# Gathering the first expert by itself and scattering expert outputs as separate partial rows, in an expert layer of a two-layer diffusion block

## The chip, the cores and the metric

The kernel runs on one core of one Trainium2 chip. The metric is the device time of one execution in microseconds; a time stands for the median of several runs.

## What is computed

Two transformer-like layers run over 256 latent and 256 context tokens of width 1024. Only the channel mixer of the second layer matters here. It is a layer of eight experts, and each of the 256 latent tokens goes to its two best:

```python
def _moe(h, router, w_gate, w_up, w_down):
    logits = (t @ router).astype(jnp.float32)
    top_val, top_idx = lax.top_k(logits, TOP_K)          # TOP_K = 2
    top_w = jax.nn.softmax(top_val, axis=-1)
    gate = jnp.sum(jax.nn.one_hot(top_idx, N_EXPERTS) * top_w[..., None], axis=1)
    for e in range(N_EXPERTS):                           # 8, each 1024 -> 3584 -> 1024
        out = out + gate[:, e:e + 1] * _swiglu(t, w_gate[e], w_up[e], w_down[e])
```

All weights are float32. The weights of the eight experts are 352 MB, and each is read once.

## The kernel before

**Stages.** Layer 0 and the mixer of layer 1 run first. From there on the code that the change touches runs: `prep_tile` (1450) computes router logits and each token's two experts for one tile of 128 tokens (the two latent tiles are `LAT = (0, 1)`); `moe_prep` (1487) computes each token's rank within each expert by matmuls with a strict triangle `tri` and with ones (lines 1495 to 1499, issued by the helper at line 1827), copies the ranks to `rk` (1501), finishes the modulated input `hf` (`modulated`, 1445 and 1448) and builds the first map; `moe_layer` (1964) does the experts; `store` (2005) writes the output.

**Gather and scatter.** `moe_map` (1527) builds, on DVE, a 0/1 map of tokens by slots for an expert: slot n holds the token whose rank is n, up to S = 96 slots. `moe_gather` (1537) handles two experts at a time. In four pieces of two blocks of 128 features it multiplies `hf` (the stationary operand, 128 columns) with the maps of both experts (192 moving columns) into a PSUM bank and copies the result to `xg` on ACT. Then it transposes each expert's map on PE (line 1564) and copies it to `ohT` on DVE (1565); the scatter uses it. A float32 matmul appears in the trace as two instructions, so a gather of 16 matmuls is 32 of them, and a pair of transposes is two.

**The expert loop.** An expert is four units. In a unit `gate_up` (1585) runs two halves of gate and up matmuls, four at a time on 32-column strips of the array (`four`, 1571), `turned` (1613) transposes the result, and `moe_down` (1631) of the unit before follows. Slots 0 to 63 are always computed. The third strip, slots 64 to 95, is computed only if the expert has more than 64 tokens; PE branches on that at run time (`arms`, 1578). So an expert with the third strip has 1.5 times the matmuls of one without. After an expert's last unit, `moe_out` (1651) scales its result into `y`, adding two partial sums for slots 64 to 95, and `moe_add` (1668) splits `y` into a high and a low part (1673, 1674), scatters both by a matmul with `ohT` (1682) and adds the result to `xt` (1684).

**Order of work.** PE's instructions in the loop are in the order of the code. Gathers and scatters wait in the queue `behind`, and `paced` (1972) lets one piece of the queue's head run after each half of `gate_up` and after each `moe_down`. Before the change the gather of experts 2 and 3 runs within expert 1, of 4 and 5 within expert 3, of 6 and 7 within expert 5; that of 0 and 1 runs ahead of the loop. On the other engines a scheduler may move instructions when the kernel is compiled.

**Weights.** `Ring` (161) holds 30 slots of 512 KB. Its loads go through SP's DMA queue, which has at most eight transfers on their way: an issue waits until the eighth transfer before it has landed. `ring.grow` (1955) issues most of the first 30 loads, as slots come free near the end of the mixer; the second `ring.grow` (1961), after `moe_prep`, issues the last two. From then on a load is issued as soon as PE is done with a slot.

Of the kernel before, what the change touches and what calls it, by code (L numbers as in the profile page):

```python
# [9 lines left out]
F32 = mybir.dt.float32  # L10
# [6 lines left out]
ALU = mybir.AluOpType  # L17
# [179 lines left out]
class Gen:  # L197
# [88 lines left out]
    def load_consts(self, cp, mp):  # L286
# [1163 lines left out]
    def prep_tile(self, tt, ws, ga):  # L1450
# [30 lines left out]
        nc.vector.tensor_copy(ixf[:, tt], ix[:, tt, 0:2])  # L1481
        nc.vector.tensor_scalar(s1[:, tt], self.iota[:, :8], ixf[:, tt, 0:1], None, op0=ALU.is_equal)
        nc.vector.tensor_scalar(o2[:, tt], self.iota[:, :8], ixf[:, tt, 1:2], None, op0=ALU.is_equal)
# [42 lines left out]

    def moe_map(self, e0, ne, sel, rank, n=S):

        oh = self.mem.get(4, [P, 2, ne, n], "oh")
# [7 lines left out]
    def moe_gather(self, e0, ne, out, sel, rank, n=S, oh=None):  # L1537

        nc, mem = self.nc, self.mem
        if oh is None:  # L1540
            oh = self.moe_map(e0, ne, sel, rank, n)
# [4 lines left out]
        o2 = mem.get(4, [P, ne, 256], "ohT", F32R)  # L1546
        left = [ne]
        for d in range(0, KD, 2):
            yield from self.avail("t")
            ps = self.psum("t")  # L1550
            for i in range(2):
                for tt in LAT:
                    self.mm(ps, ps[:, i * w:i * w + w], self.hf[tt][:, (d + i) * P:(d + i) * P + P],
                            oh[:, tt].rearrange("p a b -> p (a b)"), tt == 0, tt == 1)
            v = ps[:, :2 * w].rearrange("p (i j n) -> p i j n", i=2, j=ne)
            for j in range(ne):
                self.act(xg[j][:, d:d + 2], v[:, :, j], AF.Copy)
            self.done(ps)
            yield
        for j in range(ne):  # L1560
            yield from self.avail("t")
            ps = self.psum("t")
            for tt in LAT:
                self.last[id(ps)] = nc.tensor.transpose(ps[:n, tt * P:tt * P + P], oh[:, tt, j], self.ident)
            nc.vector.tensor_copy(o2[:n, j], ps[:n, :256])
            self.done(ps)
            out[e0 + j] = xg[j], o2[:, j], (o2, left)
            yield
        mem.put(oh)
# [61 lines left out]
    def moe_down(self, e, hT, u, yb, yx):  # L1631

        m = 4 if u < 3 else 2
        w = [(t[:, :512], t[:, 512:]) for t in self.ring.need(2 * m)]
        for arm in self.arms(e):
            if u == 0 and not arm:
                self.four(yx, 512, ((self.zero, w[0][0]),) * 4, True, True)
            for j in range(m):
                v = w[2 * j:2 * j + 2]
                for i, (w0, w1) in enumerate(v):  # L1640
                    b0, b1 = hT[:, j, i, :32], hT[:, j, i, 32:64]
                    self.four(yb, 512, ((b0, w0), (b1, w0), (b0, w1), (b1, w1)), u == 0 and j == 0 and i == 0,
                              u == 3 and j == 1 and i == 1)
                xa, xb = hT[:, j, 0, 64:], hT[:, j, 1, 64:]
                if arm:
                    self.four(yx, 512, ((xa, v[0][0]), (xa, v[0][1]), (xb, v[1][0]), (xb, v[1][1])),
                              u == 0 and j == 0, u == 3 and j == 1)
        yield
        self.mem.put(hT)

    def moe_out(self, yb, yx):

        nc, mem, gf = self.nc, self.mem, self.gf
        y, t = mem.get(4, [P, 2, 512], "y"), mem.get(4, [P, 2, 512], "yt")
        for dh in range(2):
# [3 lines left out]
        self.act(y[64:S, 1], yx[32:64], AF.Copy)  # L1659
        self.act(t[64:S, 1], yx[96:], AF.Copy)  # L1660
        nc.vector.tensor_tensor(y[64:S, 0], yx[64:S], y[64:S, 0], op=ALU.add)
        nc.vector.tensor_tensor(y[64:S, 1], t[64:S, 1], y[64:S, 1], op=ALU.add)
        self.done(yb, yx)
        nc.vector.tensor_tensor(y[64:S], y[64:S], gf[64:S].rearrange("p (a b) -> p a b", a=2), op=ALU.mult)
        mem.put(t)
        return y

    def moe_add(self, y, o, gate, n=S, free=None):
# [24 lines left out]

    def moe_rest(self):

        nc, tc = self.nc, self.tc
        with tc.For_i(0, NE, 1) as e:
            for off, n in ((S, P), (S + P, 256 - S - P)):
                with tc.If(nc.values_load(self.cnt[0:1, bass.ds(e, 1)], min_val=0, max_val=256) > off):
                    self.moe_rest_expert(bass.ds(e, 1), off, n)  # L1700

    def moe_rest_expert(self, one, off, n):
# [6 lines left out]
        xg = {}  # L1709
        self.run(self.moe_gather(0, 1, xg, *cols[:2], n))  # L1710
        x, o, free = xg[0]
# [124 lines left out]
    def build(self):  # L1836
        nc, tc, A = self.nc, self.tc, self.A
        with ExitStack() as ctx:
# [125 lines left out]
    def moe_layer(self):  # L1964
# [13 lines left out]
        def lower():  # L1978
# [5 lines left out]
            if u == 3:  # L1984
                behind.append(self.moe_add(self.moe_out(*y), xg[e][1], self.gate[:, :, e:e + 1], S, xg[e][2]))
# [19 lines left out]
    def store(self):  # L2005
        for tt in LAT:
            for z in range(2):
                s = slice(512 * z, 512 * z + 512)
# [27 lines left out]
def _consts():  # L2036
# [5 lines left out]
    for lv in range(7):  # L2042
# [75 lines left out]
```

## Time and profile before

| | |
|---|---|
| runs | 1835.87, 1839.38, 1839.55 us; median 1839.38 |
| the profiled execution | 1835.17 us |
| its span, first to last instruction | 1833.4 us |
| before the first expert matmul | 936.3 us |
| expert loop, first to last expert matmul | 878.9 us |
| after the last expert matmul | 18.2 us |

PE is TensorE's matmuls, PEld its weight loads, DVE is VectorE, ACT is ScalarE, SP is the engine that issues the DMAs. Times of the trace count from the span's start. The granted clock is the share of 2.4 GHz that TensorE got.

### The profile page before, as it was taken

To read this page: it belongs to the slowest core of one execution; us is meant where nothing else is said; L and a number is where in the kernel's file an instruction comes from. 1 tells how busy PE (TensorE), PEld (TensorE's weight loads), DVE (VectorE), ACT (ScalarE), POOL (GpSimd) and SP (SyncE) were. 2 spreads that over 40 slices of the span, in tenths; PEclk is the share of its full clock that TensorE was granted. 3 is DMA by queue.
4 is the path that set the end of the run, shared out by engine and by line. 5 is a ranking of instruction groups with operands and counts; after the bars stand their busy time and mean duration, and the time that the engine had idled before them with its cause. 6 is when DMAs were issued, how large, how long until landed. Compare 5 with 4: busy or idle time off the path is not lost. (4 is left out here: it accounts for less than half of the span.)

```text
span 1833.4 us, 34728 instructions
## 1 busy us (share of the span) xinstructions
PE 1753.2 (96%) x14056; PEld 1084.3 (59%) x14057; DVE 778.5 (42%) x1924; ACT 537.7 (29%) x1203; POOL 33.3 (2%) x56
## 2 busy tenths in 40 slices
PE   6999999999999999999989998999989999999996
PEld 3999778988788898998843333333333333333332
DVE  4656877899755377868720011110212011120112
ACT  4654655723223256765410010100101011010100
POOL 1000000100000001000000000000000000000000
PEclk9999999999999999999989999999999999999998
DMA  9224342366763245230589999999999999999990
GB/s 347 73 83 147 114 150 80 117 241 226 240 221 134 97 143 182 89 127 13 196 316 379 402 406 407 406 407 400 402 400 406 404 402 402 400 407 404 403 392 31
DMA packets 137006, 485.64 MB, mean 265 GB/s; under 512 B 15888, under 2 KB 17040, under 8 KB 136784
## 3 DMA queue, kind: packets, MB, share of 16 engines
q1 hardware_dynamic: 136080, 480.08, 69.1%
q8 instruction: 168, 2.75, 0.6%
q0 software_dynamic: 704, 2.36, 0.4%
q14 instruction: 54, 0.44, 0.1%
HBM read 481.33 MB, written 1.05 MB: 263 GB/s over the span
## 5 line engine op out<-in xcount | busy, mean ns | idle before, releaser
L1575 PE MATMUL u<-wr,xg 128*32 128x512 f32 (+1 forms) x5376 | 523.9, 545 | 19.7 <-issue 14.6
L1575 PEld LDWEIGHTS u<-wr,xg 128*32 128x32 f32 x5376 | 174.0, 111 | 342.2 <-issue 291.5
L1575 PE MATMUL mm<-wr,mT 128*32 128x512 f32 x2352 | 261.1, 593 | 3.8 <-ACT mh L264 1.5
L125 ACT ACTIVATE hi<-raw 128x512 fp32r<-128x512 f32 (+2 forms) x296 | 160.3, 580 | 247.1 <-PE u L246 84.8
L126 DVE TENSOR_TENSOR lo<-raw,hi 128x512 fp32r<-128x512 f32 (+2 forms) x296 | 178.9, 636 | 98.3 <-ACT hi L125 96.7
L1608 DVE TENSOR_TENSOR mh<-mh,u 128x512 f32<-128x512 f32 (+1 forms) x32 | 19.8, 619 | 410.9 <-PE u L1575 257.0
L1575 PEld LDWEIGHTS mm<-wr,mT 128*32 128x32 f32 x2352 | 77.8, 110 | 175.4 <-issue 149.7
L264 ACT ACTIVATE mh<-u 128x512 f32<-128x512 f32 (+1 forms) x64 | 34.6, 540 | 413.9 <-PE u L1575 413.3
L244 PE MATMUL u<-hx,hi 128*128 128x512 f32 (+1 forms) x384 | 142.9, 372 | 0.0
L245 PE MATMUL u<-hx,lo 128*128 128x512 f32 (+1 forms) x384 | 142.7, 372 | 0.0
L246 PE MATMUL u<-hx,hi 128*128 128x512 f32 (+1 forms) x384 | 142.7, 372 | 0.0
L264 ACT ACTIVATE mT<-t 128x512 f32<-128x512 f32 (+1 forms) x32 | 17.4, 544 | 256.3 <-PE t L1620 255.4
L245 PE MATMUL mm<-fx,lo 128*128 128x256 f32 (+1 forms) x264 | 85.7, 325 | 4.4 <-DVE lo L126 4.2
L244 PE MATMUL mm<-hi,hx 128*128 128x256 f32 x288 | 85.3, 297 | 4.2 <-ACT hx L264 3.9
L244 PE MATMUL mm<-fx,hi 128*128 128x256 f32 (+1 forms) x264 | 85.0, 322 | 0.6 <-ACT hi L125 0.6
L1626 DVE COPY mT<-t 128x256 f32<-128x256 f32 (+1 forms) x32 | 12.5, 392 | 170.6 <-PE t L1625 170.6
L246 PE MATMUL mm<-fx,hi 128*128 128x256 f32 (+1 forms) x264 | 84.6, 321 | 0.0
L245 PE MATMUL mm<-hi,hx 128*128 128x256 f32 x288 | 82.0, 286 | 0.6 <-DVE hx L521 0.3
L246 PE MATMUL mm<-lo,hx 128*128 128x256 f32 x288 | 81.7, 285 | 0.2 <-DVE lo L126 0.2
L246 PEld LDWEIGHTS u<-hx,hi 128*128 128x128 f32 x384 | 72.4, 188 | 12.6
L245 PEld LDWEIGHTS u<-hx,lo 128*128 128x128 f32 x384 | 72.4, 188 | 12.4
L244 PEld LDWEIGHTS u<-hx,hi 128*128 128x128 f32 x384 | 72.4, 188 | 12.4
(342 smaller groups left out, 2624.9 us busy)
## 6 DMA issues: line engine op xcount, KB each, us to landing
wr<-in_moe_g SPq DMA_DIRECT2D x224, 512.0 KB, 10.1
wr<-in_moe_u SPq DMA_DIRECT2D x224, 512.0 KB, 10.1
wr<-in_moe_d SPq DMA_DIRECT2D x224, 512.0 KB, 10.1
adat<-in_w_adaT SPq DMA_DIRECT2D x56, 512.0 KB, 5.0
raw<-in_ffn_gu SPq DMA_DIRECT2D x44, 512.0 KB, 3.5
adaw<-in_w_ada SPq DMA_DIRECT2D x40, 512.0 KB, 6.5
raw<-in_w_in SPq DMA_DIRECT2D x40, 512.0 KB, 3.5
raw<-in_ffn_d SPq DMA_DIRECT2D x24, 384.0 KB, 3.6
```

The lines of the kernel that those rows point to most:

```text
L125: nc.scalar.activation(h[:, s], r[:, s], AF.Copy)
L126: nc.vector.tensor_tensor(l[:, s], r[:, s], h[:, s].bitcast(F32), op=ALU.subtract)
L244: i = mm(ps, lh, rh, start=start, stop=False, skip_group_check=True)
L245: mm(ps, ll, rh, start=False, stop=False, skip_group_check=True)
L246: self.final = mm(ps, lh, rl, start=False, stop=stop, skip_group_check=True)
L264: i = self.nc.scalar.activation(out, in_, func, **kw)
L1575: self.nc.tensor.matmul(bank[c:c + 32, :n], lhsT, rhs, start=start, stop=stop, tile_position=(0, c), skip_group_check=True)
L1608: nc.vector.tensor_tensor(h[:, 0, :n], h[:, 0, :n], U[:, :n], op=ALU.mult)
L1626: nc.vector.tensor_copy(hT[:, :m, :, 64:], pt[:, :m * 64].rearrange("p (j a s) -> p j a s", j=m, a=2))
```

## The change

`tri` is no longer loaded at the start but on SP's queue behind the first `ring.grow`, into a slot of the ring's memory that is given back after the rank matmuls, and `ring.grow` takes one slot fewer there and one more later. The constant `iota` becomes `slots`, 256 wide, in which the slots 64 to 95 appear three times: the map of an expert now has 256 columns, of which the first 96 gather; as two maps of 128 columns it scatters, one for each half of the features, and in each the partial sums of slots 64 to 95 stand in two rows that the matmul adds. So each expert's map needs two pairs of transposes. `moe_out` is four multiplies, `moe_add` splits `y` by halves. The gathers are now 0 alone ahead of the loop (its transposes go into the loop), 1 and 2 within expert 0, 3 and 4 within expert 2, 5 and 6 within expert 4, 7 alone within expert 6. `store` writes by halves of the features. `moe_rest`, for experts with more than 96 tokens, is changed to match and isn't executed with these inputs.

```diff
@@ load_consts
-        self.router, self.tri = ld("router", [P, KD, 8]), ld("tri", [P, P])
-        self.iota = ld("iota", [P, P])
+        self.router = ld("router", [P, KD, 8])
+        self.slots = ld("slots", [P, 2 * P])
@@ moe_prep
         mm(2, self.ones, 1, False, True)
+        mem.put(self.tri)
+        for tt in LAT:
+            self.modulated(tt, sh, sc)
         rk = t_("rk", [P, 3, 8])
         nc.vector.tensor_copy(rk, pr[:, :24].rearrange("p (a b) -> p a b", a=3))
         self.done(pr)
-
         self.sel, self.rank = s2, rk
-        for tt in LAT:
-            self.modulated(tt, sh, sc)
-        self.map0 = self.moe_map(0, 2, s2, rk)
+        self.map0 = self.moe_map(*self.GATHERS[0], s2, rk, self.slots)
@@ moe_map, moe_gather
+    GATHERS = ((0, 1), (1, 2), (3, 2), (5, 2), (7, 1))
+
+    def moe_map(self, e0, ne, sel, rank, pos):
+        oh = self.mem.get(4, [P, 2, ne, pos.shape[1]], "oh")
...
-                self.nc.vector.tensor_scalar(oh[:, tt, j], self.iota[:, :n], rank[:, tt, e:e + 1], sel[:, tt, e:e + 1],
+                self.nc.vector.tensor_scalar(oh[:, tt, j], pos, rank[:, tt, e:e + 1], sel[:, tt, e:e + 1],
...
+        rows = min(P, pos.shape[1])
+        nm = pos.shape[1] // rows
         yield
         w = ne * n
+        per = min(KD, 512 // w // 2 * 2)
...
-        for d in range(0, KD, 2):
+        for d in range(0, KD, per):
...
             for j in range(ne):
-                self.act(xg[j][:, d:d + 2], v[:, :, j], AF.Copy)
+                if ne == 1 and d:
+                    nc.vector.tensor_copy(xg[j][:, d:d + per], v[:, :, j])
+                else:
+                    self.act(xg[j][:, d:d + per], v[:, :, j], AF.Copy)
             self.done(ps)
+            if d + per >= KD:
+                out.update(got)
             yield
         for j in range(ne):
...
+            for i in range(nm):
+                yield from self.avail("t")
+                ps = self.psum("t")
+                for tt in LAT:
+                    self.last[id(ps)] = nc.tensor.transpose(ps[:rows, tt * P:tt * P + P],
+                                                            oh[:, tt, j, i * rows:i * rows + rows], self.ident)
+                nc.vector.tensor_copy(o2[:rows, j, i], ps[:rows, :256])
+                self.done(ps)
             yield
@@ moe_down
-                    self.four(yx, 512, ((xa, v[0][0]), (xa, v[0][1]), (xb, v[1][0]), (xb, v[1][1])),
+                    self.four(yx, 512, ((xa, v[0][1]), (xb, v[1][1]), (xa, v[0][0]), (xb, v[1][0])),
@@ moe_out
-        y, t = mem.get(4, [P, 2, 512], "y"), mem.get(4, [P, 2, 512], "yt")
+        y = mem.get(4, [P, 2, 512], "y")
         for dh in range(2):
-            r, s = slice(64 * dh, 64 * dh + 64), slice(512 * dh, 512 * dh + 512)
-            nc.vector.tensor_tensor(y[:64, dh], yb[r], gf[r, s], op=ALU.mult)
-        self.act(y[64:S, 0], yx[:32], AF.Copy)
...
-        nc.vector.tensor_tensor(y[64:S], y[64:S], gf[64:S].rearrange("p (a b) -> p a b", a=2), op=ALU.mult)
+            for r, src in ((slice(0, 64), (yb, yx)[dh]), (slice(64, P), (yx, yb)[dh])):
+                nc.vector.tensor_tensor(y[r, dh], src[r], gf[r, 512 * dh:512 * dh + 512], op=ALU.mult)
@@ moe_add
-        self.act(yh[:n], y[:n], AF.Copy)
-        nc.vector.tensor_tensor(yl[:n], y[:n], yh[:n].bitcast(F32), op=ALU.subtract)
+        for dh in range(2):
+            self.act(yh[:n, dh], y[:n, dh], AF.Copy)
+            nc.vector.tensor_tensor(yl[:n, dh], y[:n, dh], yh[:n, dh].bitcast(F32), op=ALU.subtract)
...
+                om = o[:n, dh % o.shape[1], tt * P:tt * P + P]
                 for z, t in enumerate((yh, yl)):
-                    nc.tensor.matmul(ps, o[:n, tt * P:tt * P + P], t[:n, dh], start=(z == 0), stop=(z == 1))
+                    nc.tensor.matmul(ps, om, t[:n, dh], start=(z == 0), stop=(z == 1))
@@ build
-            self.ring.grow(len(mem.free[4]) - 5)
+            self.ring.grow(len(mem.free[4]) - 6)
+            self.tri = mem.get(4, [P, P], "tri")
+            nc.sync.dma_start(self.tri, A["tri"])
@@ moe_layer
-        self.run(self.moe_gather(0, 2, xg, self.sel, self.rank, S, self.map0))
-        behind = deque()
+        first = self.moe_gather(*self.GATHERS[0], xg, self.sel, self.rank, oh=self.map0)
+        while 0 not in xg:
+            next(first)
+        behind = deque([first])
...
-                if u == 0 and e % 2 and e + 1 < NE:
-                    behind.append(self.moe_gather(e + 1, 2, xg, self.sel, self.rank))
+                if u == 0 and e + 1 in dict(self.GATHERS):
+                    behind.append(self.moe_gather(e + 1, dict(self.GATHERS)[e + 1], xg, self.sel, self.rank))
@@ store
-        for tt in LAT:
-            for z in range(2):
+        for z in range(2):
+            for tt in LAT:
@@ _consts
-                iota=f(np.broadcast_to(np.arange(P), (P, P))),
+                slots=f(np.broadcast_to(np.r_[0:96, 64:96, 64:96, 64:96, 0:64], (P, 2 * P))),
```

## Rows read from the trace of the kernel before

**Rows 1.** Busy time by stretch: from 920 us to the last expert matmul.

```profile
core 0: us, PE busy (x) PEld busy (x) DVE busy (x) ACT busy (x) POOL busy (x), PEclk, DMA share, GB/s
920.00:930.00 10.00, 6.25 (x26) 6.04 (x26) 7.07 (x35) 1.09 (x4) 0.00 (x0) 0.54 1.01 406
930.00:936.30 6.30, 5.54 (x31) 5.00 (x30) 0.92 (x4) 2.57 (x9) 0.00 (x0) 0.91 0.90 360
936.30:1815.20 878.90, 847.16 (x8140) 299.09 (x8140) 112.11 (x181) 78.53 (x149) 0.00 (x0) 0.99 0.98 385
```

**Rows 2.** PE in the loop, 936.3 to 1815.2 (count, busy us, mean ns, idle).

```profile
L1575 PE MATMUL u<-wr,xg 128*32 128x512 f32 (+1 forms) x5376 | 523.9, 545 | 19.7 <-issue 14.6 <-DMA wr<-in_moe_g 4.3 <-DMA wr<-in_moe_d 0.6
...
L1827 PE MATMUL t<-oh,mhf 128*128 128x192 f32 x96 | 18.8, 339 | 0.0
...
L1564 PE MATMUL t<-ident,oh 128*96 128x128 f32 x12 | 2.5, 293 | 0.0
```

**Rows 3.** PE's timeline (start, length, line, count, [idle before]), ranks to first expert.

```profile
924.10 0.60 PE L1827 MATMUL t<-s,tri 128*128 128x8 f32 x2 [1.18 <-DVE s L1484]
...
924.55 1.43 PE L1827 MATMUL t<-s,ones 128*128 128x8 f32 x6
...
927.86 7.03 PE L1827 MATMUL t<-oh,mhf 128*128 128x192 f32 x32 [1.89 <-DVE oh L1533]
...
936.30 20.81 PE L1575 MATMUL u<-wr,xg 128*32 128x512 f32 x192 [0.34 <-issue]
```

**Rows 4.** Timeline of DVE between the choice of experts and the first gather.

```profile
923.96 1.28 DVE L1445 SCALAR_TENSOR_TENSOR mhf<-xt,mrs,sc 128x1024 f32<-128x1024 f32 x1
926.01 0.18 DVE L1501 COPY rk<-t 128x24 f32<-128x24 f32 x1 [0.77 <-PE t L1827]
926.11 1.22 DVE L1448 TENSOR_TENSOR mhf<-mhf,sh 128x1024 f32<-128x1024 f32 x1
927.24 1.05 DVE L1533 TENSOR_SCALAR oh<-iota,rk,s 128x96 f32<-128x96 f32 x4
```

**Rows 5.** SP issues around the gather; landing time, issues of 917 to 932.

```profile
923.19 1.60 SPq L179 DMA_DIRECT2D wr<-in_moe_u  x2
925.79 1.61 SPq L179 DMA_DIRECT2D wr<-in_moe_g  x2
...
wr<-in_moe_g SPq DMA_DIRECT2D x6, 512.0 KB, 10.1
```

**Rows 6.** The gather's weight loads, by form, from 1000 us on.

```profile
L1827 PEld LDWEIGHTS t<-oh,mhf x96: 186/190/191, 1061.6 to 1523.5; 128*128 128x128 f32 x96
```

**Rows 7.** PE's timeline around a gather within the loop.

```profile
1061.59 1.57 PE L1827 MATMUL t<-oh,mhf 128*128 128x192 f32 x8
1063.08 5.36 PE L1575 MATMUL mm<-wr,mT 128*32 128x512 f32 x48
...
1071.79 0.66 PE L1620 MATMUL t<-ident,mh 128*128 128x128 f32 x4 [1.85 <-DVE mh L1608]
```

**Rows 8.** What PE waited for in the loop: total us, times, longest.

```profile
PE t L1620 <- DVE mh L1608: 6.5, 4, 1.9
PE u L1575 <- DMA wr<-in_moe_g: 4.3, 2, 3.8
```

**Rows 9.** Timeline behind the last expert matmul.

```profile
1815.27 1.39 DVE L1657 TENSOR_TENSOR y<-mm,gf 64x512 f32<-64x512 f32 x2 [5.30 <-PE mm L1575]
...
1818.48 1.22 DVE L1664 TENSOR_TENSOR y<-y,gf 32x1024 f32<-32x1024 f32 x1
1819.73 1.06 ACT L264 ACTIVATE yhl<-y 96x1024 fp32r<-96x1024 f32 x1 [2.60 <-DVE y L1664]
1820.82 1.22 DVE L1674 TENSOR_TENSOR yhl<-y,yhl 96x1024 fp32r<-96x1024 f32 x1 [1.12 <-ACTq L2001]
...
1823.73 2.08 PE L1682 MATMUL t<-yhl,ohT 96*128 96x512 f32 x4 [0.42 <-DVE xt L1684]
...
1824.99 1.60 DVE L1684 SCALAR_TENSOR_TENSOR xt<-t,gate,xt 128x512 f32<-128x512 f32 x2 [0.66 <-PE t L1682]
```

More of the change, by code (lines that the diff above doesn't have):

```diff
@@ L1481, in prep_tile @@
         nc.vector.tensor_copy(ixf[:, tt], ix[:, tt, 0:2])
-        nc.vector.tensor_scalar(s1[:, tt], self.iota[:, :8], ixf[:, tt, 0:1], None, op0=ALU.is_equal)
-        nc.vector.tensor_scalar(o2[:, tt], self.iota[:, :8], ixf[:, tt, 1:2], None, op0=ALU.is_equal)
+        nc.vector.tensor_scalar(s1[:, tt], self.slots[:, :8], ixf[:, tt, 0:1], None, op0=ALU.is_equal)
+        nc.vector.tensor_scalar(o2[:, tt], self.slots[:, :8], ixf[:, tt, 1:2], None, op0=ALU.is_equal)
         self.chosen = nc.vector.tensor_tensor(s2[:, tt], s1[:, tt], o2[:, tt], op=ALU.add)
@@ L1525, in moe_prep @@
         mem.put(sh, sc)
-    def moe_map(self, e0, ne, sel, rank, n=S):
-        oh = self.mem.get(4, [P, 2, ne, n], "oh")
+    GATHERS = ((0, 1), (1, 2), (3, 2), (5, 2), (7, 1))
+    def moe_map(self, e0, ne, sel, rank, pos):
+        oh = self.mem.get(4, [P, 2, ne, pos.shape[1]], "oh")
         for tt in LAT:
@@ L1532, in moe_map, with moe_gather @@
                 e = e0 + j
-                self.nc.vector.tensor_scalar(oh[:, tt, j], self.iota[:, :n], rank[:, tt, e:e + 1], sel[:, tt, e:e + 1],
+                self.nc.vector.tensor_scalar(oh[:, tt, j], pos, rank[:, tt, e:e + 1], sel[:, tt, e:e + 1],
                                              op0=ALU.is_equal, op1=ALU.mult)
         return oh
-    def moe_gather(self, e0, ne, out, sel, rank, n=S, oh=None):
+    def moe_gather(self, e0, ne, out, sel, rank, n=S, oh=None, pos=None):
         nc, mem = self.nc, self.mem
+        pos = self.slots if pos is None else pos
@@ L1540, in moe_gather @@
         if oh is None:
-            oh = self.moe_map(e0, ne, sel, rank, n)
+            oh = self.moe_map(e0, ne, sel, rank, pos)
+        rows = min(P, pos.shape[1])
+        nm = pos.shape[1] // rows
         yield
         w = ne * n
+        per = min(KD, 512 // w // 2 * 2)
         yield from mem.room(4, ne + 1)
         xg = [mem.get(4, [P, KD, n], "xg") for _ in range(ne)]
-        o2 = mem.get(4, [P, ne, 256], "ohT", F32R)
+        o2 = mem.get(4, [P, ne, nm, 256], "ohT", F32R)
         left = [ne]
-        for d in range(0, KD, 2):
+        got = {e0 + j: (xg[j], o2[:, j], (o2, left)) for j in range(ne)}
@@ L1549, in moe_gather @@
+        for d in range(0, KD, per):
             yield from self.avail("t")
             ps = self.psum("t")
-            for i in range(2):
+            v = ps[:, :per * w].rearrange("p (i j n) -> p i j n", i=per, j=ne)
+            for i in range(per):
                 for tt in LAT:
-                    self.mm(ps, ps[:, i * w:i * w + w], self.hf[tt][:, (d + i) * P:(d + i) * P + P],
-                            oh[:, tt].rearrange("p a b -> p (a b)"), tt == 0, tt == 1)
-            v = ps[:, :2 * w].rearrange("p (i j n) -> p i j n", i=2, j=ne)
+                    self.mm(ps, v[:, i], self.hf[tt][:, (d + i) * P:(d + i) * P + P], oh[:, tt, :, :n], tt == 0, tt == 1)
@@ L1563, in moe_gather @@
-            for tt in LAT:
[L1564 to L1567, printed above, removed]
+            for i in range(nm):
[6 more added lines that the diff above has]
+                self.done(ps)
@@ L1653, in moe_out, with moe_add @@
         nc, mem, gf = self.nc, self.mem, self.gf
-        y, t = mem.get(4, [P, 2, 512], "y"), mem.get(4, [P, 2, 512], "yt")
+        y = mem.get(4, [P, 2, 512], "y")
         for dh in range(2):
-            r, s = slice(64 * dh, 64 * dh + 64), slice(512 * dh, 512 * dh + 512)
-            nc.vector.tensor_tensor(y[:64, dh], yb[r], gf[r, s], op=ALU.mult)
-        self.act(y[64:S, 0], yx[:32], AF.Copy)
[L1659 to L1662, printed above, removed]
+            for r, src in ((slice(0, 64), (yb, yx)[dh]), (slice(64, P), (yx, yb)[dh])):
+                nc.vector.tensor_tensor(y[r, dh], src[r], gf[r, 512 * dh:512 * dh + 512], op=ALU.mult)
         self.done(yb, yx)
-        nc.vector.tensor_tensor(y[64:S], y[64:S], gf[64:S].rearrange("p (a b) -> p a b", a=2), op=ALU.mult)
-        mem.put(t)
         return y
-    def moe_add(self, y, o, gate, n=S, free=None):
+    def moe_add(self, y, o, gate, n=P, free=None):
         nc, mem = self.nc, self.mem
@@ L1697, in moe_rest @@
         with tc.For_i(0, NE, 1) as e:
-            for off, n in ((S, P), (S + P, 256 - S - P)):
+            for off, n in ((S, S), (2 * S, 256 - 2 * S)):
                 with tc.If(nc.values_load(self.cnt[0:1, bass.ds(e, 1)], min_val=0, max_val=256) > off):
@@ L1709, in moe_rest_expert @@
         xg = {}
-        self.run(self.moe_gather(0, 1, xg, *cols[:2], n))
+        self.run(self.moe_gather(0, 1, xg, *cols[:2], n, pos=self.slots[:, :n]))
         x, o, free = xg[0]
@@ L1984, in lower @@
             if u == 3:
-                behind.append(self.moe_add(self.moe_out(*y), xg[e][1], self.gate[:, :, e:e + 1], S, xg[e][2]))
+                behind.append(self.moe_add(self.moe_out(*y), xg[e][1], self.gate[:, :, e:e + 1], P, xg[e][2]))
         with tc.manual_schedule(engines={mybir.EngineType.PE}):
             for e, u in self.UNITS:
-                if u == 0 and e % 2 and e + 1 < NE:
-                    behind.append(self.moe_gather(e + 1, 2, xg, self.sel, self.rank))
+                if u == 0 and e + 1 in dict(self.GATHERS):
+                    behind.append(self.moe_gather(e + 1, dict(self.GATHERS)[e + 1], xg, self.sel, self.rank))
                 h = mem.get(4, [P, 2, 512], "mh")
@@ L2005, in store @@
     def store(self):
-        for tt in LAT:
-            for z in range(2):
+        for z in range(2):
+            for tt in LAT:
                 s = slice(512 * z, 512 * z + 512)
```

2 lines of the change are left out of this document (removed).

## The prediction, made before the kernel was run

> **What bounds the kernel now.** I read the time by stretch first. In the expert loop, 878.9 of the span's 1833.4 us, PE has instructions for 847.2 us, DVE for 112 and ACT for 79 [rows 1]. The DMA engines are busy for 0.98 of it too, so two things compete for the bound, and the waits decide: within the loop PE's longest kind of wait for weights comes to 4.3 us in 2 times, less than the 6.5 us that it waited for DVE's `mh` [rows 8]. So I take PE as the bound of the loop, with the weight stream close behind; work that is added to PE's queue there lengthens the kernel, and work on DVE and ACT beside it doesn't. The groups of PE's instructions give the price of what the change multiplies: 96 gather instructions for 18.8 us, three gathers, so 6.27 us each; 12 transposes for 2.5 us, six pairs, 0.42 us each [rows 2]. Before the loop a chain decides: ranks on PE, rank copy and map on DVE, gather on PE, first expert matmul at 936.30 [rows 3, 4]. Behind the loop a second chain takes the last 18.2 us [rows 9]. These two chains are where the change saves; the loop is where it pays.
>
> **Loop: one gather more, ten pairs of transposes more.** Before, three gathers and six pairs run within the loop. After, four gathers (the last for expert 7 alone) and eight experts by two pairs do. A gather for one expert has as many matmuls as one for two: each is one weight load of 128 columns of `hf` for 96 instead of 192 moving columns. A gather's weight load takes 190 ns [rows 6], and eight instructions take 1.57 us, 196 ns each [rows 7]: the weight load sets the spacing, and it stays. So the fourth gather costs the full 6.3 us, the ten pairs 4.2 us, less 0.08 us by which each of 14 pieces overlaps its neighbour (eight instructions of 1.57 us from 1061.59, the next at 1063.08 [rows 7]), 1.0 us: +9.5 us.
>
> The Trainium skill, page "TensorE: Matmul & The Clock Gate", section "Back-to-back issue gap", gives a spacing of N/2.4 + 2.5 ns for an isolated stream, which is 42.5 ns for 96 columns, 1.4 us for a gather of 32 instructions. By that the fourth gather would cost 1.4 instead of 6.3 us and the gather ahead of the loop 5.6 us less, and the total would be some 10 us lower than mine; the 196 ns of the rows decide against it.
>
> Each of the three gathers in the loop also shows one stall of 1.85 us: the second piece's copies stand ahead of the unit's activation on ACT, and PE's transposes wait for `mh` [rows 7, 8]. Four gathers bring four such stalls if nothing else changes, +1.85 us; none of them would be -5.55 us. I take +1.85, as every gather shown has one. In the loop: +11.35 us, between +4 and +13.
>
> **Start, if the triangle is in time.** Three things are removed ahead of the first expert matmul. `modulated` no longer stands behind the rank copy: DVE sat idle for 0.77 us before line 1501 and did 1.22 us of line 1448 behind it, with the map at 927.24 [rows 4]. With line 1448 right behind line 1445, at 925.2, it ends at 926.4, the rank copy (ready at 925.98) and the map follow, 926.5. A 256-wide map lies between 0.33 us (128x96: four in 1.05) and 0.69 us (a multiply of 512 columns) [rows 4, 9]; I take 0.5. First gather matmul 927.05 instead of 927.86. The gather keeps its 7.03 us (16 weight loads, doubled) [rows 3]. The two pairs of transposes leave, and DVE's copy of 384 columns, 0.33 to 0.69 us, I take 0.6 with its semaphore, comes between: first expert matmul at 934.7, 1.55 us earlier. The loads ahead of it don't matter for that: 30 are issued before.
>
> **Start, with the triangle where the diff puts it.** The load of `tri` was long done before. Now SP issues it behind the loads of the first `ring.grow`. That growth's last load was the second of the pair at 923.19, so issued about 924.46 [rows 5]; the diff takes one load off the growth, and `tri` gets its place. Loads of that time land 10.1 us after their issue [rows 5], since up to eight stand before them in the queue and 406 GB/s are already moved [rows 1]. The load ahead, of 923.19, lands at about 933.4; `tri` follows with 64 KB, 0.16 us: 933.6. The first matmul with `tri` that mattered stood at 924.10 [rows 3]. What is queued behind it on PE: all rank matmuls, the gather and the experts; on DVE, `rk`, the map, the copies. From 933.65: 0.5 us for tile 0's triangle, which had been done ahead, 1.9 us to the rank copy (924.10 to 926.01), copy 0.2, map 0.55, gather 7.0, copy 0.6: first expert matmul at 944.5, +8.2 us. Line 1448 is no part of it any more. The granted clock was 0.54 from 920 to 930 us and 0.91 after [rows 1], that is half speed while PE waited for the ranks and then full speed; a longer wait may prolong the half-speed part, up to +1.5 us. Bounds of the late case: +7.5 and +9.7.
>
> Which of the two holds is the largest single choice. A scheduler could hoist `tri`; but its slot is memory of the mixer's constants, as is that of the last ten or so loads of that growth, and these are issued at once, in the code's order, from 915 on. So late is my choice.
>
> The wait moves the loop's start, and the weights too: the ring is full at 30 loads until the first expert's matmuls free a slot, so landings move by as much as PE does. Inside expert 0 the ring is still full, and the extra pieces there delay the stream by some 9 us; that is paid once PE has spent its lead over the stream in an expert without third strip, and PE has by then spent 11 us more itself. I count nothing for it; up to +2 us.
>
> **End.** From the last matmul (1815.2) DVE does 1.39 us of multiplies, ACT copies, two additions, a multiply of 1.22, then ACT 1.06, DVE 1.22 and eight matmuls with four DVE steps to 1826.59 [rows 9]. After: four multiplies of 0.69, done at 1818.05; the first half's high part on ACT runs beside the last two; its subtraction, half of 1.22, is done at 1818.7 instead of the whole at 1822.04. From there it was 4.55 us to the last step; the end of the chain moves to 1823.25, -3.35 us; say -3.5, because matmuls with the high part are done earlier. With full clock in these matmuls -4.3; if DVE's order puts both subtractions last, -2.5. The store's last transfer follows the last step as before.
>
> **What costs nothing.** `moe_out`'s other seven rounds, wider maps, the second copy of each map on DVE: DVE is busy 112 of 879 us, and PE's matmuls cover them [rows 1]; without that cover each scatter would wait some 1 us. The order of the third strip in `moe_down` has the same number of matmuls. Stores by halves wait for the same last step. `moe_rest` doesn't run.
>
> **Sum.** +8.2 + 11.35 - 3.5 = +16.0 us. Against the profiled execution's own 1835.17 us that is 1851.2. The runs have a median 4.2 us higher, 1855.4; I put the forecast between the two bases, 1837.3 + 16.0 = **1853**. A measurement of this kernel can tell some 0.2%, 3.7 us, from no change.
>
> **Rivals.** *The triangle is in time* (hoisted on SP, or overtaking the loads): -1.55 + 11.35 - 3.5 = +6.3, 1843.6 us. For it: a scheduler orders SP's queue. Against: the order of rows 5 and the 10.1 us. Chance 0.20.
>
> *The weight stream is the bound*, and the change is faster. For it: DMA share 0.98 at 385 GB/s over the whole loop [rows 1]. Then PE's 11 us fill time in which it would have waited for weights anyway, and only the two chains count: with `tri` in time -1.55 - 3.5 = -5.05, 1832.2 us. It decides from the point where PE waits for weights for more than about 11 us in the loop; the rows show 4.3 as the largest kind. With `tri` late it gives +4.7, 1842.0. Chances 0.08 and 0.05.
>
> The Trainium skill, page "Trainium Kernel Development and Optimization", section "Performance Expectations", warns that matmul busy time says little of a bound, because matmuls are pipelined, and names weight-load busy time instead; that is 299 of 879 us here, and by it PE would not be the bound. The waits of rows 8 speak against.
>
> *The change doesn't do what it says*: the scheduler leaves DVE's order at start and end as it was. That gives back some 1 us at either end, within the range.
>
> **How the numbers follow.** Forecast case 0.62, with its own range of 1846 to 1858: the loop at its lower bound with weights in the way takes off 7, clock and contention add 4. Triangle in time 0.20, 1840 to 1847. Stream-bound 0.13. The rest, 0.05, is unknown. The range 1840 to 1859 leaves out the faster case and little above. Faster by over 0.2% (below 1835.7): 0.09. Within: the stream-bound case with `tri` late and a part of the triangle in time, 0.14. Slower: 0.77.
>
> **What would show it.** Right: SP issues `tri` near 924.5 and it lands near 933.6; PE's rank matmuls wait for a DMA there; first expert matmul near 944.5; in the loop 128 gather instructions for about 25 us and 32 transposes for about 6.7; last matmul to last DVE step 8 us instead of 11.4. Wrong: `tri` issued before 916; a gather of 96 columns in half the time; a loop that is no longer than 879 us.

## The result, and the profile after

The kernel before has a median of 1838.72 us over 6 runs (1835.87 to 1839.55), the changed one 1868.92 us over 6 (1866.43 to 1869.99): a ratio of 1.0165, 95% interval 1.0152 to 1.0178. It is slower, as forecast, but by 30 us where the forecast was 16 and the range ended at 1859. In the profiled executions the span goes from 1833.4 to 1865.0 us, +31.6:

| stretch | before | after | difference | forecast |
|---|---|---|---|---|
| up to the first expert matmul | 936.30 | 943.64 | +7.3 | +8.2 |
| expert loop | 878.90 | 907.41 | +28.5 | +11.35 |
| last expert matmul to the end | 18.2 | 13.95 | -4.25 | -3.5 |

Start and end came out close to their terms; the loop holds nearly the whole error. First the start, PE's timeline of the changed kernel from the last router matmuls on:

```profile
start us, us, engine line op out<-in xcount [idle before <-releaser]
922.89 1.18 PE L1836 MATMUL t<-rsc,mxT 128*128 128x8 f32 x8 [0.69 <-ACT mxT L264]
936.13 0.99 PE L1836 MATMUL t<-s,tri 128*128 128x8 f32 x4 [12.06 <-DMA tri<-in_tri]
936.97 1.43 PE L1836 MATMUL t<-s,ones 128*128 128x8 f32 x6
939.12 4.58 PE L1836 MATMUL t<-oh,mhf 128*128 128x96 f32 x20 [0.72 <-DVE oh L1535]
943.64 0.87 PE L1588 MATMUL u<-wr,xg 128*32 128x512 f32 x4
```

and SP's issues of that time:

```profile
922.96 1.62 SPq L179 DMA_DIRECT2D wr<-in_moe_g  x2
925.53 0.33 SPq L179 DMA_DIRECT2D wr<-in_moe_u  x1
926.80 0.33 SPq L1966 DMA_DIRECT2D tri<-in_tri  x1
```

The triangle is issued at 926.80, behind all loads of that growth, and PE stands idle for it for 12.06 us, until 936.13. That answers to the 1.18 us of idle time at 924.10 in [rows 3]. Only 20 of the gather's 32 matmuls run ahead of the first expert matmul; the other 12 follow behind its first half.

Now the loop. PE's groups there (count, busy us, mean ns, idle before them and what ended it), which answer to [rows 2]:

```profile
L1588 PE MATMUL u<-wr,xg 128*32 128x512 f32 (+1 forms) x5376 | 528.9, 546 | 24.3 <-issue 15.7 <-DMA wr<-in_moe_g 8.4
L1588 PE MATMUL mm<-wr,mT 128*32 128x512 f32 x2352 | 264.3, 596 | 7.7 <-issue 6.6 <-DMA wr<-in_moe_g 0.9 <-ACT mT L264 0.2
L1836 PE MATMUL t<-oh,mhf 128*128 128x192 f32 (+1 forms) x141 | 24.9, 321 | 0.0
L1633 PE MATMUL t<-ident,mh 128*128 128x128 f32 x112 | 19.2, 288 | 11.4 <-DVE mh L1621 9.3 <-DVE xt L1693 1.5 <-DVE ohT L1579 0.6
...
L1577 PE MATMUL t<-ident,oh 128*128 128x128 f32 x32 | 5.4, 287 | 0.4 <-DVE xg L1565 0.4
```

The forecast work is there: gathers 18.8 to 24.9 us, transposes of maps 2.5 to 5.4, waits for `mh` 6.5 to 9.3, together +11.8. The rest, 16.7 us, sits in the expert matmuls, whose number nobody changed: they are busy for longer (523.9 to 528.9 in gate and up, 261.1 to 264.3 in down) and PE idles more before them (19.7 to 24.3 and 3.8 to 7.7). Most of that idle time ends with "issue". What the profile puts down to weights there is not a lack of them: the loads for the second half of expert 1's first unit had landed 29 us before PE began it, after a wait of 2.20 us put down to them (landing times in the trace against PE's matmuls), and no matmul of the loop started less than 7 us behind its weights. In the kernel before, none started less than 6 us behind them either, so its 4.3 us in [rows 8] were no lack of weights.

Where it sits is seen by expert. Microseconds from each expert's first gate matmul to the next one's, from PE's timeline (experts 0, 2, 4, 6 and 7 have the third strip):

| expert | 0 | 1 | 2 | 3 | 4 | 5 | 6 | 7 |
|---|---|---|---|---|---|---|---|---|
| before | 110.3 | 98.8 | 116.6 | 101.0 | 116.3 | 99.4 | 115.6 | 120.9 |
| gathers before (0-1 ahead) | | 2-3 | | 4-5 | | 6-7 | | |
| after | 122.9 | 100.0 | 126.0 | 93.5 | 126.5 | 93.1 | 124.7 | 120.9 |
| gathers after (0 ahead) | 1-2 | | 3-4 | | 5-6 | | 7 | |

A gather that moves in costs an expert with third strip 9 to 13 us. A gather that moves out gives expert 1 nothing back (98.8 to 100.0), and 3 and 5 only 7.5 and 6.3 us. Expert 1 without a gather still takes 100 us, of which PE is busy for 88.3, at a granted clock of 0.95 (time by stretch, changed kernel):

```profile
core 0: us, PE busy (x) PEld busy (x) DVE busy (x) ACT busy (x) POOL busy (x), PEclk, DMA share, GB/s
943.64:1851.05 907.41, 863.20 (x8205) 310.67 (x8204) 110.97 (x194) 68.42 (x136) 0.00 (x0) 0.99 0.95 373
1066.50:1166.50 100.00, 88.30 (x798) 32.68 (x796) 14.78 (x26) 7.70 (x15) 0.00 (x0) 0.95 1.01 396
```

and in the kernel before, with the gather in it:

```profile
1046.60:1145.40 98.80, 90.83 (x836) 33.88 (x840) 14.93 (x23) 11.13 (x24) 0.00 (x0) 0.98 1.03 406
```

The end (all engines, changed kernel), answering to [rows 9]:

```profile
1851.12 2.81 DVE L1671 TENSOR_TENSOR y<-mm,gf 64x512 f32<-64x512 f32 x4 [5.30 <-PE mm L1588]
1852.55 0.63 ACT L264 ACTIVATE yhl<-y 128x512 fp32r<-128x512 f32 x1 [6.90 <-DVE y L1671]
...
1853.97 1.36 DVE L1682 TENSOR_TENSOR yhl<-y,yhl 128x512 fp32r<-128x512 f32 x2
...
1857.48 1.60 DVE L1693 SCALAR_TENSOR_TENSOR xt<-t,gate,xt 128x512 f32<-128x512 f32 x2 [0.72 <-PE t L1691]
```

Four multiplies of 0.7 us, halves on ACT beside them, last DVE step done at 1859.1, 8.0 us behind the last matmul (1851.05), as the prediction said it would be.

### The profile page after: what moved, and what is told of

It is laid out like the page before. It is cut to its first block, busy times and chain, and to the rows that moved or that the text cites. A ratio compares the mean times of both kernels' runs of the same rounds, so it can differ in the third digit from the quotient of the medians.

```text
span 1865.0 us, 34813 instructions
## 1 busy us (share of the span) xinstructions
PE 1767.7 (95%) x14104; PEld 1094.4 (59%) x14105; DVE 774.3 (42%) x1934; ACT 523.9 (28%) x1181; POOL 33.8 (2%) x56
## 4 chain that ended last, share of the span: by engine, by line
PE 77%; DMA 9%; DVE 7%; issue 3%; ACT 3%; SPq 0%; POOL 0%; DVEq 0%; ACTq 0%; POOLq 0%
PE u L1588 26%; PE mm L1588 13%; PE u L244 5%; PE u L245 5%; PE u L246 5%; PE u L1836 4%; PE mm L244 3%; PE mm L245 3%; PE mm L246 3%; DMA wr<-in_moe_g 3%; DMA adat<-in_w_adaT 2%; PE u L860 2%; PE t L1836 2%; DMA wr<-in_moe_d 2%; PE u L395 2%
## 5 line engine op out<-in xcount | busy, mean ns | idle before, releaser
L1588 PE MATMUL u<-wr,xg 128*32 128x512 f32 (+1 forms) x5376 | 528.9, 546 | 24.3 <-issue 15.7
L1588 PE MATMUL mm<-wr,mT 128*32 128x512 f32 x2352 | 264.3, 596 | 7.7 <-issue 6.6
L1588 PEld LDWEIGHTS mm<-wr,mT 128*32 128x32 f32 x2352 | 81.6, 110 | 176.6 <-issue 160.1
L244 PE MATMUL mm<-fx,hi 128*128 128x256 f32 (+1 forms) x264 | 85.9, 326 | 0.5 <-ACT hi L125 0.5
L245 PEld LDWEIGHTS u<-hx,lo 128*128 128x128 f32 x384 | 72.3, 188 | 12.6
```

The lines of the kernel that those rows point to most:

```text
L244: i = mm(ps, lh, rh, start=start, stop=False, skip_group_check=True)
L245: mm(ps, ll, rh, start=False, stop=False, skip_group_check=True)
L1588: self.nc.tensor.matmul(bank[c:c + 32, :n], lhsT, rhs, start=start, stop=stop, tile_position=(0, c), skip_group_check=True)
```

## The experiments

The theory was: **PLACE**, PE stalls for instructions in the experts without third strip, so a gather there costs little, and moving it into experts with third strip costs it in full. Rivals: **WORK**, the new transposes, the 128-row scatter and the wider maps cost it; **STREAM**, the weights do. Ratios are to runs of the kernel before on the same chip, whose medians were 1838.2 to 1839.3 us.

**1. The triangle alone.** The changed kernel with

```diff
-            self.ring.grow(len(mem.free[4]) - 6)
             self.tri = mem.get(4, [P, P], "tri")
             nc.sync.dma_start(self.tri, A["tri"])
+            self.ring.grow(len(mem.free[4]) - 5)
```

> The changed kernel with the load of the triangle ahead of the ring's growth on SP instead of behind it. All theories of the loop: the loop stays at about 907 us; the rank matmuls no longer wait for a DMA, so the first expert matmul moves from 943.6 to 934 to 936 and the time from 1869 to 1860 or 1861. If the wait for the triangle was only in front of another one, the first expert matmul stays above 940.

1856.96 us, ratio 1.0093 (1.0076 to 1.0110): 12 us less than the changed kernel, where 8 or 9 were expected. Its four times lie between 1854.9 and 1864.3 us, and the profile is of the longest. PE's timeline:

```profile
924.26 1.06 PE L1836 MATMUL t<-rsc,mxT 128*128 128x8 f32 x8 [0.69 <-ACT mxT L264]
925.17 0.37 PE L1836 MATMUL t<-s,tri 128*128 128x8 f32 x2
926.92 0.60 PE L1836 MATMUL t<-s,tri 128*128 128x8 f32 x2 [1.38 <-DVE s L1484]
927.37 1.43 PE L1836 MATMUL t<-s,ones 128*128 128x8 f32 x6
930.52 6.72 PE L1836 MATMUL t<-oh,mhf 128*128 128x96 f32 x32 [1.73 <-DVE oh L1535]
937.17 1.06 PE L1588 MATMUL u<-wr,xg 128*32 128x512 f32 x8
```

The wait is gone and nothing of its size stands behind it: from the last router matmuls to the first expert matmul it is 12.9 us instead of 20.75, with all 32 gather matmuls in it. This run's mixer ended 1.4 us later, so the first expert matmul came at 937.2, not at 934 to 936. The loop stayed long, at 910.4. (From the last router matmuls to the first expert matmul the kernel before takes 15.6 us: in time, the triangle makes the start 2.7 us shorter, where the prediction had 1.55.)

**2. The schedule alone, undone and done.** The changed kernel with the gathers as pairs, at their old places:

```diff
-    GATHERS = ((0, 1), (1, 2), (3, 2), (5, 2), (7, 1))
+    GATHERS = ((0, 2), (2, 2), (4, 2), (6, 2))
```

> The changed kernel with the gathers put back to four pairs, in the experts 1, 3 and 5 that have no third strip; all else stays. Theory PLACE (a gather among the matmuls of an expert without third strip costs little, because PE stalls for instructions there anyway, and its full price and more among those of one with it): the loop falls from 907 us to 882 to 886, the first gather grows by some 2.5 us, the time is about 1847. Rival WORK (the missing 17 us are the added transposes, the 128-row scatter and the wider maps, wherever the gathers stand): only the fourth gather and its stall go, 8 us, the time is about 1863. Rival STREAM (the expert's extra pieces delay the weights, and PE waits for them later): between the two, with waits for weights in the loop gone that are there in the changed kernel.

1843.90 us, ratio 1.0031 (1.0021 to 1.0041): 25.0 us come back, and the loop is 883.8 us. PLACE, not WORK: all that the other parts of the change add in the loop is 4.9 us. Nor STREAM: in the changed kernel no matmul had to wait for its weights, as the landing times showed. Its groups of expert matmuls, busy and idle:

```profile
L1588 PE MATMUL u<-wr,xg 128*32 128x512 f32 (+1 forms) x5376 | 521.9, 541 | 16.6 <-issue 11.3 <-DMA wr<-in_moe_g 5.1
L1588 PE MATMUL mm<-wr,mT 128*32 128x512 f32 x2352 | 261.1, 593 | 7.4 <-issue 4.6 <-DMA wr<-in_moe_g 1.9 <-DMA wr<-in_moe_d 0.6
```

The other way round, the kernel before with only the schedule changed:

```diff
-        self.map0 = self.moe_map(0, 2, s2, rk)
+        self.map0 = self.moe_map(0, 1, s2, rk)
...
-                if u == 0 and e % 2 and e + 1 < NE:
-                    behind.append(self.moe_gather(e + 1, 2, xg, self.sel, self.rank))
+                if u == 0 and e % 2 == 0:
+                    behind.append(self.moe_gather(e + 1, min(2, NE - 1 - e), xg, self.sel, self.rank))
```

> The kernel before with nothing changed but the schedule of the gathers: expert 0 alone, then the pairs 1-2, 3-4, 5-6 in the experts 0, 2, 4 and expert 7 alone in 6. PLACE: the loop grows by 22 to 26 us from 879, the time is 1858 to 1863. WORK: it grows by the fourth gather and its stall alone, 8 us, 1845.

1867.62 us, ratio 1.0151 (1.0134 to 1.0168): +28.8 us, more than PLACE expected (the loop is 914.8 us, +35.9 in its profile). The schedule alone makes the kernel as slow as the whole change. In this profile experts 1, 3 and 5 take 98.3, 100.3 and 102.8 us without a gather in them, where they took 98.8, 101.0 and 99.4 with one: here nothing comes back at all. Why the changed kernel got 7.5 and 6.3 us back in 3 and 5 and this one nothing stays open.

**3. Where the stalls come from: the branch over the third strip.** The two arms are fixed when the program is written, as this input needs them, in the changed kernel and in the one before (these kernels hold for this input alone):

```diff
     def arms(self, e):
-        with self.tc.If(self.third[e] > 0) as c:
-            yield 1
-        with c.Else():
-            yield 0
+        yield (1, 0, 1, 0, 1, 0, 1, 1)[e]
```

> The changed kernel with the experts' two arms decided when the program is written (third strip in 0, 2, 4, 6 and 7, as this input has it), so that no branch stands in the loop. PLACE: the stalls that end with 'issue' inside the runs of expert matmuls go, the loop falls from 907 us by 20 to 30, the time is 1840 to 1850. STREAM: the loop stays within 5 us of 907, with the waits now shown as waits for weights. If stalls come from the count of instructions and not from the branch, the loop stays too, but the waits remain 'issue'.

1833.72 us, ratio 0.9969 (0.9956 to 0.9981), loop 872.5 us: time and loop are 6 and 5 us below the ranges of PLACE. Not one wait for "issue" is left among the expert matmuls; now they wait for weights, in many short waits:

```profile
L1588 PE MATMUL u<-wr,xg 128*32 128x512 f32 (+1 forms) x5376 | 525.8, 540 | 7.4 <-DMA wr<-in_moe_u 7.1
L1588 PE MATMUL mm<-wr,mT 128*32 128x512 f32 x2352 | 264.8, 594 | 4.8 <-DMA wr<-in_moe_d 4.3 <-ACT mT L264 0.2
```

Expert 1, with the same matmuls as in the changed kernel, takes 81.7 us instead of 100, and PE is busy in all of it:

```profile
1066.22:1147.92 81.70, 81.32 (x798) 28.15 (x796) 15.12 (x27) 7.07 (x14) 0.00 (x0) 1.00 1.02 403
```

So 18.3 us of expert 1 were stalls and what they brought: 11.3 us more of idle time, and 7.0 us more of busy time for the same matmuls. Behind the longer stalls PE ran for some microseconds at about half its clock (0.57 of 2.4 GHz from 1094.84 to 1098.26, after 2.70 us of idle time); by the mean of 0.95 over 100 us, that is an estimated 5 of the 7.0 us.

Expert 1 is the clearest place, not the only one. Of the 35 us by which the loop is shorter, 18.3 are in expert 1, 15.8 in experts 0, 2, 4 and 6 together (117.1, 121.3, 124.6 and 121.3 us now), and 1.1 in 3 and 5. Expert 3, in the changed kernel and with fixed arms:

```profile
1292.50:1385.90 93.40, 83.69 (x797) 28.63 (x796) 14.78 (x26) 7.68 (x15) 0.00 (x0) 1.00 1.03 407
1269.30:1361.77 92.47, 87.17 (x799) 26.60 (x797) 15.13 (x27) 7.15 (x14) 0.00 (x0) 1.00 1.03 409
```

Its idle time ended with "issue" before, and with fixed arms it ends with weights, 4.8 us in 17 short waits: once PE comes earlier, the weights are not there yet.

Is it the jump, or the code that is jumped over? Two kernels have fixed arms in the experts with third strip, and in 1, 3 and 5 a jump that skips either the whole other arm or, in the second kernel, one group of four matmuls in its place:

```diff
-        with self.tc.If(self.third[e] > 0) as c:
-            yield 1
-        with c.Else():
-            yield 0
+        if e in (1, 3, 5):
+            with self.tc.If(self.third[e] > 0):
+                yield 1
+            yield 0
+        else:
+            yield 1
```

> The changed kernel with the arms fixed for the experts 0, 2, 4, 6 and 7 (no branch there), and in 1, 3 and 5 a branch over the arm with third strip, which is never taken, ahead of the arm without it: the same matmuls as in the run with fixed arms, plus jumps over 96 matmuls each. Theory VOLUME (PE stalls because the instructions that it skips have to be brought in as well, so the stall grows with the code that is jumped over): the stalls of the experts 1, 3 and 5 come back, expert 1 takes 96 to 100 us as with both arms (82 with fixed arms), the loop 888 to 900 us, the time 1848 to 1862. Theory BRANCH (each jump has its price, whatever it skips): the same here as in the next run with small arms.

> As the run before, with the same number of jumps in the experts 1, 3 and 5, each over 4 matmuls only instead of 96 (32 to 96 in the shorter blocks). VOLUME: next to no stall, expert 1 takes 82 to 84 us, loop 872 to 876, time 1833 to 1838 as with fixed arms. BRANCH: expert 1 as in the run with long arms, 96 to 100 us.

With long arms 1838.85 us (ratio 0.9991, 0.9976 to 1.0006), loop 878.5, expert 1 92.6 us; with short ones 1832.85 us (0.9963, 0.9950 to 0.9976), loop 872.8, expert 1 85.6, still 3.9 more than with no jump at all. VOLUME holds against BRANCH: with the same number of jumps the waits behind the jump (line 1594 on PE's sequencer) are 0.2 or 0.3 us at the longest with short arms,

```profile
PE u L1588 <- PEq L1594: 2.2, 12, 0.2
PE mm L1588 <- PEq L1594: 1.7, 5, 0.3
```

and up to 2.8 us with long ones:

```profile
PE u L1588 <- PEq L1594: 8.3, 13, 2.8
PE mm L1588 <- issue: 3.9, 2, 2.0
PE mm L1588 <- PEq L1594: 3.6, 4, 2.2
```

But the long arms cost less than expected (expert 1 92.6, not 96 to 100; loop and time 9 us below their ranges). What they lack against the changed kernel is the second arm in the experts with third strip; so PE, it seems, comes into expert 1 already behind when those have two arms; a run with two arms in those alone was not made. Nor do these two runs tell whether PE waits for all of the skipped code or only for the piece that the jump leads to: a jump over more code also leads further on.

The profile shows the code itself, as packets of the queue named "instruction" (packets, MB, share). Within expert 1, in the changed kernel:

```profile
q8 instruction: 15, 0.25, 1.0%
```

in the changed kernel with fixed arms:

```profile
q8 instruction: 6, 0.10, 0.5%
```

with long skipped arms:

```profile
q8 instruction: 15, 0.25, 1.1%
```

and with short ones:

```profile
q8 instruction: 7, 0.11, 0.5%
```

So code that is skipped is brought in like code that runs, in packets of some 16 KB (0.25 MB in 15). In the changed kernel and in the one before every expert takes 14 to 16 packets. Those with third strip need some 110 us or more for their work anyway. Expert 1 needs 82 us for its work, but took 100 for its 15 packets in the changed kernel and 92.6 for 15 with long skipped arms, 6.7 and 6.2 us for each. In 3 and 5 no such price can be read: they took 93.5 and 93.1 us with 15 packets and, held up by weights, 92.5 and 93.0 with 6. The Trainium skill, page "Runtime: NRT & Kernel Launch", section "Instruction fetch mechanics", says that instructions arrive in blocks of 16 KiB in sequence, and that a taken branch to a target outside of what is at hand stalls the engine. Size and stall agree with these rows; that skipped blocks are transferred too, beside a stream of weights that fills the DMA engines (share 1.01 in expert 1), is what the runs add.

The kernel before with fixed arms shows what a gather costs where it can't hide:

> The kernel before with the two arms fixed when the program is written, nothing else. VOLUME: without stalls to hide in, a gather in expert 1 costs its full price: expert 1 takes 89 to 92 us, where the changed kernel with fixed arms had 82 without a gather; the loop falls from 879 to 865 to 871 us and the time to 1824 to 1832. If the kernel before had no such stalls to lose, its time stays within 4 us of 1839.

1820.40 us, ratio 0.9900 (0.9883 to 0.9916); loop 863.1 us, time and loop 4 and 2 us below the expected ranges; expert 1 takes 89.2 us, 7.5 more than without a gather. Between the two kernels with fixed arms the loop differs by 9.4 us (863.1 to 872.5), not by 28.5.

**4. Run-time branches with little to skip.** The matmuls that both arms share are written once, outside; under the branch stands the third strip alone (the zeroing of its bank, for the experts without it, is done for all):

```diff
-            for arm in self.arms(e):
-                for q in range(2):
...
-                        if arm:
-                            self.four(X, n, ((b2, ga), (b2, gb), (b2, ua), (b2, ub)), *z)
+            for q in range(2):
...
+                    third.append((((b2, ga), (b2, gb), (b2, ua), (b2, ub)), z))
+            with self.tc.If(self.third[e] > 0):
+                for parts, z in third:
+                    self.four(X, n, parts, *z)
```

and in the same way in `moe_down`. Four kernels have it: the changed one; with the triangle first and pairs as well; the one before; the changed one with the triangle first.

> The changed kernel, run-time branches kept, but the matmuls that both arms have are written once, outside, and only those of the third strip stand under the branch: an expert without it skips 32 matmuls per half instead of 96, one with it skips none. Same number of branches. VOLUME: expert 1 falls from 100 to 82 to 88 us, the loop from 907 to 876 to 885, the time to 1838 to 1847. BRANCH: loop within 5 us of 907, time 1864 to 1869.

> The same with the triangle loaded first and the gathers as four pairs in the experts 1, 3 and 5. VOLUME: first expert matmul at 936 to 938, the loop 868 to 876 (the weight stream limits it, as in the run with fixed arms), behind it 14 us, time 1820 to 1830, faster than both kernels. BRANCH: as the run with pairs less the 9 to 12 us of the triangle, 1832 to 1835.

> The kernel before with the matmuls that both arms share written outside the branch, as in the runs of the changed kernel. VOLUME: loop 868 to 874 us, time 1827 to 1834. Against the same version with the change's tail and maps, the triangle first and the pairs (1824.2), what is left between the two is the change's own gain behind the loop less its transposes: 2 to 5 us. BRANCH: within 4 us of 1839.

> The changed kernel, its own gather schedule, with the shared matmuls outside the branch and the triangle first. VOLUME: where few stalls are left, the place of a gather matters little, and the schedule costs only its fourth gather and stall, 6 to 9 us against the run with pairs (1824.2): 1830 to 1834. PLACE alone, whatever the branches: the schedule costs 25 us here too, 1849.

| | us | ratio, interval | loop | expert 1 |
|---|---|---|---|---|
| changed | 1841.43 | 1.0016 (1.0002 to 1.0031) | 882.6 | 85.9 |
| changed, triangle first, pairs | 1824.21 | 0.9910 (0.9880 to 0.9940) | 873.2 | 92.9 |
| before | 1827.41 | 0.9934 (0.9917 to 0.9950) | 872.3 | 91.9 |
| changed, triangle first | 1834.08 | 0.9974 (0.9962 to 0.9986) | 882.6 | 85.9 |

Nearly all as VOLUME expected, the last at the edge of its range. In the loop, the instruction queue moves for the changed kernel (and as much for the one before)

```profile
q8 instruction: 120, 1.97, 0.9%
```

and with shared matmuls outside

```profile
q8 instruction: 74, 1.21, 0.6%
```

27.5 us go with these 46 packets. The count alone doesn't give the time: the long skipped arms moved 91 packets in a loop of 878.5 us, these kernels 74 in 882.6. Here PE also zeroes the bank for all experts, 8.3 us of matmuls instead of 3.2. The schedule, which cost 25.0 us with two full arms, costs 9.9 here (1834.08 against 1824.21, on two chips; by the ratios 11.8). The second row beats both kernels. It is 3.2 us below the third, also on two chips; the intervals of the ratios overlap, so that the change's other parts, its shorter end less its transposes, bring something on balance is likely but not shown.

**5. Both costs taken out** (the edits of 1 and 2 together, both arms as they were):

> The changed kernel with both parts undone that cost time: gathers as four pairs in the experts 1, 3 and 5, and the triangle loaded first; partial rows, four multiplies and the last scatter in halves stay. If the two costs add up (each worked out from its own run): 1843.9 less 10 to 12 us, 1832 to 1835, below the kernel before by 4 to 7 us. If the loop absorbs an earlier start, because the weights then limit it: 1838 to 1843.

1836.17 us, ratio 0.9984 (0.9972 to 0.9996), 1 us above the expected sum. The triangle is worth 7.7 us here, 7.4 with shared matmuls outside and 12.0 in experiment 1, whose four times spread over 9 us; beyond that no reason for the difference was found.

## Why the prediction was right, and where it was wrong

**Start: right.** The triangle comes late, as forecast. Its price was forecast as 9.75 us (+8.2 against -1.55 in time) and measured as 7 to 12 us by three pairs of runs. SP issued it at 926.8 instead of 924.5, and PE went on 9.3 us after that (9.2 in the prediction's step). That +7.3 came so near +8.2 is in part luck, as two misses cancel: 2.2 us of it come from the mixer, whose last router matmuls start at 922.89 instead of 920.71 (in other runs with a late triangle at 919.54 to 926.09), and 12 gather matmuls were moved behind the first half. The granted clock stayed at 0.50 to the end of the gather (936.13 to 943.64), the longer half-speed part that the prediction held possible.

**End: right**, -4.25 against -3.5, the upper bound being -4.3. The chain to the last DVE step is 3.4 us shorter (11.4 to 8.0), as worked out; the other 0.9 us lie behind it, where no difference was expected, and the whole end varies by as much between profiles with the same code there (13.9 to 15.0 us in the changed kernel and experiments 1, 2 and 5).

**Loop: wrong by 17 us, and by one step:** "So the fourth gather costs the full 6.3 us ... +9.5 us" priced only the gather that is added. The three others were taken as unchanged, because their matmuls are. But the change moves them, from experts where PE stalled for instructions (idle for 6 to 9 us each before) into experts where it hardly did (1.4 to 2.5). The kernel's order of work names both places; no step of the prediction asked what each place cost. By the table of experts, the moves into 0, 2, 4 and 6 cost 12.6, 9.4, 10.2 and 9.1 us; out of 1, 3 and 5 come -1.2, 7.5 and 6.3: 41.3 - 12.6 = 28.7, the loop's +28.5 but for rounding. (The 12.6 of expert 0 hold the 12 moved matmuls of its own gather and its transposes, too.)

Which side failed shows when the prediction's own prices are put beside these numbers. Arriving, the gathers with their transposes, stalls and the 12 moved matmuls (1.6 us) come to 12.2, 9.8, 9.8 and 9.0 us, 40.8 against 41.3 measured. Leaving, each should have given back 6.27 + 0.84 + 1.85 = 9.0 us, 27 together; 12.6 came back. Of the 14.4 us that didn't, 10.2 are expert 1's.

The row that could have told it stood in [rows 2]: idle time of 19.7 us before the gate matmuls, "issue 14.6". It was PE's largest kind of wait in the loop:

```profile
PE u L1575 <- issue: 14.6, 12, 3.4
```

The prediction compared waits for weights (4.3) with waits for `mh` (6.5) and left this one out. It took PE's work as the bound of the whole loop, where in experts 1, 3 and 5 PE also stood still for lack of instructions.

Where little code is skipped, the loop's term is about right: +9.4 us between the kernels with fixed arms, +10.3 between those with shared matmuls outside (872.3 to 882.6), against +11.35. There the weights limit a part of the loop, so these are no pure prices of PE's work either.

**The price of the fourth gather was too high, too.** "The weight load sets the spacing, and it stays", 196 ns. Expert 7's gather, changed kernel:

```profile
1626.25 2.02 PE L1836 MATMUL t<-oh,mhf 128*128 128x96 f32 x16
1632.16 2.02 PE L1836 MATMUL t<-oh,mhf 128*128 128x96 f32 x16
```

That is 126 ns each, 4.0 us instead of 6.3; the columns count. The rule weighed there, of the Trainium skill's page "TensorE: Matmul & The Clock Gate", section "Back-to-back issue gap" (42.5 ns for 96 columns), is off by more on the other side; the section gives it for a single matmul by itself, not for a stream of matmuls with weight loads as here. That all gathers of the loop still grew by 6.1 us, near the 6.3, is luck: the 12 matmuls moved in from the start add 1.6. The added stalls were right in kind: waits for `mh` went from 6.5 to 9.3 us, +2.8 for the +1.85.

**The rivals.** The triangle in time: no. The weight stream as the bound: not in this kernel, but it stood right behind: as soon as the stalls were gone, PE waited for weights (11.4 us with fixed arms), and 863 us is the shortest loop that any run showed, with the DMA engines busy for 0.99 of it. That PE's work would be hidden was right of expert 1 and in part of 3 and 5, by another cause.

## What to carry to other kernels

Before a piece of work is moved, ask at each of the two places what ends the engine's idle time, stretch by stretch; "issue" is an answer, and may be the largest. Under a run-time branch put only what differs: what is skipped is brought in like what runs, and the instruction queue's packets, counted by stretch, show it. A load that a short chain needs goes ahead of a bulk of loads on its queue, not behind.

## What was not expected of the hardware

With an unchanged count of matmuls, expert 1 took 82 us when only the code that runs was there, 92.6 us with a long skipped arm in 1, 3 and 5, and 100 us with two arms in every expert. The instruction queue moved 0.25 instead of 0.10 MB for that, beside 39 MB of weights: 1.0% of the DMA engines' time. The stalls also brought half-speed stretches that cost PE an estimated 5 us in expert 1. Whether a packet of code waits behind weights in the DMA engines was not tried; no run took the weight stream away.
